# A depthwise convolution as three half-rate filters, written over its own input, on VectorE beside a matmul stream

## The chip, the cores and the metric

The kernel runs on one core of a Trainium2 chip. The metric is the device time of one execution in microseconds (us). Before the change three runs took 2227.54, 2218.27 and 2216.67 us; the median is 2218.27 us.

## The reference, cut to what matters

One layer on a sequence of 2048 frames with 1024 channels, all in float32: a norm, a combined input projection, two branches, a gated merge, an output projection and an MLP. The convolution sits in branch B.

```
proj = rmsnorm(x) @ w_in
u_pool, u_glu, g_a, g_b = split(proj)
branch_a = pool_mixer(u_pool, ...)            # trailing means, small matmuls
v = a * sigmoid(gate)                         # a, gate: halves of u_glu, 512 channels each
v = depthwise_conv(v, conv_w, width 31, causal) + conv_b
branch_b = silu(layernorm(v)) @ w_conv_out
merged = sigmoid(g_a) * branch_a + sigmoid(g_b) * branch_b
x = x + rmsnorm(merged @ w_o)
x = x + rmsnorm(relu(rmsnorm(x) @ w_up)^2 @ w_down)
```

Depthwise means that each channel has its own 31 taps: y[n] is the sum over k of w[k] times v[n + k], on a v with 30 zeros in front.

## The kernel before

Channels lie on the 128 partitions and frames along the free dimension. The sequence is two blocks (b = 0, 1) of 1024 frames. The large matmuls take each float32 operand as a high and a low part (`split`, `split_w`: ScalarE rounds the high part, VectorE subtracts) and multiply octets of blocks with seven products in place of eight (`Octet`), so VectorE also adds and subtracts weights and cells (`ws`, `wl`, `tr`, `big` in the profile), and adds matmul results that lie in PSUM to a held copy (`block_out`, L119 to L116 in the profile; for instance `tr<-ga,tr`). There are three PSUM buffers for the main products (`ps_mm`). A product that needs a buffer, or an accumulator, that such an addition still reads has to wait for it.

TensorE runs one main line of products: input projection of block 0 (glu, pool, ga, gb), branch A of block 0, input projection of block 1, branch B and `wo` of block 0, branch A of block 1, the MLP's `up` of block 0, then the same rest for block 1 and the `down` products.

Everything else is background work in `Lane` objects. After each product the main line calls `bg()`, and each lane takes `rate` steps of its generators. The convolution is such a generator (`conv_steps`, L896): for each of four channel groups c of a block it loads a window `v` of 1054 frames from DRAM (`vd`), then runs 31 taps on VectorE over 1024 frames, one instruction per tap and one step per tap, into an accumulator `acc` in a one-buffer pool `p_y` (named `y` in the profile). It stores `acc` to `yd`, adds it to `sums`, and goes on. That is 32 steps a group, and eight groups in all: group 0 of block 0 beside glu, pool and ga of block 0, the others up to the MLP's `up` of block 0. The pool branch (`pool_steps`) uses the same two buffers of `v` windows. Each of SyncE's loads and stores (`load`, L125) stands in one queue in program order.

The instruction order of each engine is settled when the kernel is built: a scheduler places the background instructions between those of the main line, by priorities (`tc.high_priority`) and by an order that `behind()` and `marks` tie to the main line. An engine runs its own list strictly in order.

Of the kernel before, what the change touches and what calls it, by code (L numbers as in the profile page):

```python
# [8 lines left out]
F32 = mybir.dt.float32  # L9
# [6 lines left out]
P = 128  # L16
D = 1024
SEQ = 2048
T = 512
# [24 lines left out]
C_MPRE = 32  # L44
C_MPOST = 40
C_CNT = 48
C_CW = C_CNT + 4 * HALO
NCONST = C_CW + CC * TAPS


# [15 lines left out]
def block_kernel(  # L66
# [35 lines left out]
    def mk(pl, tag, dt=F32, shape=(P, TB)):  # L102
        return pl.tile(list(shape), dt, tag=tag, name=nm(tag))
# [79 lines left out]
    inv_d = p_const.tile([P, 1], F32, tag="invd", name="inv_d")  # L183
    nc.gpsimd.memset(inv_d, 1.0 / D)
    inv_c = p_const.tile([P, 1], F32, tag="invc", name="inv_c")
    nc.gpsimd.memset(inv_c, 1.0 / CW)


# [705 lines left out]

    sums, done = {}, set()

    def conv_steps(b, groups, ahead=True):


        def get(c):  # L900
            v = window(TAPS - 1 + TB)
            load(v, vd[c][:, b * TB : b * TB + TAPS - 1 + TB])
            return v

        v = None
        for c in groups:
            if v is None:
                v = get(c)
                yield 1
            nv = None  # L910
            acc = mk(p_y, "y")
            for k in range(TAPS):
                wk = col(C_CW + c * TAPS + k)
                if k == 0:
                    nc.vector.tensor_scalar(
                        acc, v[:, :TB], wk, col(C_CB + c), op0=ALU.mult, op1=ALU.add
                    )
                else:
                    nc.vector.scalar_tensor_tensor(  # L919
                        acc, v[:, k : k + TB], wk, acc, op0=ALU.mult, op1=ALU.add  # L920
                    )
                if ahead and k == 15 and c != groups[-1]:
                    nv = get(c + 1)
                yield
            v = nv
            if c == 0:
                sums[b] = mk(p_ss, "sm")
                nc.vector.tensor_copy(sums[b], acc)
            else:
                add(sums[b], sums[b], acc)  # L930
            load(yd[b, c, 0], acc)
            yield

    def norm_steps(b, lag):
# [68 lines left out]
    def pool_steps(b, alone):  # L1003

        def get(g):
            s, u = window(W), tr()
            load(s, ud[g][:, b * TB : b * TB + W])
            load(u, ud[g][:, HALO + b * TB : HALO + b * TB + TB])
            return s, u

        s, u = get(0)
        yield 1
        for g in range(CC):
            w, m = WINDOWS[g], 1
            while m < w:
                lo = HALO - (w - 2 * m)
                s2 = window(W) if alone or m in (2, 8) else mk(p_ss, "r", F32, (P, W))
                add(s2[:, lo:], s[:, lo:], s[:, lo - m : W - m])
                s, m = s2, 2 * m
                yield  # L1020
            if b == 0:
                mul(
                    s[:, HALO : HALO + w],
                    s[:, HALO : HALO + w],
                    cst[:, C_CNT + g * HALO : C_CNT + g * HALO + w],
                )
# [502 lines left out]

    clear_halos()  # L1530
    opening()
    tail = Lane(1.9, conv_steps(0, (0,)))
    stats = Lane(1, in_stats(1))

    def then(f, o, at=4):
# [9 lines left out]
        return o  # L1545

    def after_glu():
        ahead[0] = AHEAD
        lanes.append(tail)

    def more():
        pool_weight()
        tail.gens.append(chain_of(pool_steps(0, True), conv_steps(0, (1, 2, 3), False)))
        tail.rate = 3

    pi = pool_in(0, parts)[0]
    run_first(o1, then(lambda: lanes.append(stats), then(after_glu, o2, 6)), bg, dve)
# [18 lines left out]
        yield from gen  # L1576

    rest = [marked(chain_of(*rest), "conv")]
    lanes += [Lane(3.2, *rest, marked(norm_steps(0, 1), "norm"))]

    def pooling():
        lanes[0].rate = 2.8
        lanes.append(Lane(1.7, pool_steps(1, False)))
        lanes.append(Lane(1.5, behind_all(conv_steps(1, (0, 1, 2, 3)), "conv", ("windows", 1))))


    pi = pool_in(1, parts)[0]
# [10 lines left out]
    lanes.append(conv1)  # L1598
    merged = merge(0, bg)
    fetched = []  # L1600
    conv1.rate = 6
    parts = Parts(lambda ops: token_parts(ops, lambda c, t: parts.raw(c, t), *BIG, TR))
    chain = out_proj(
        0, merged, ((0,), (1,)), bg, parts.some, lambda: fetched.extend(fetch_spread(mxd, 1))
# [487 lines left out]
```

## Time and profile before

| what | value |
|---|---|
| profiled execution, its own time | 2218.92 us |
| its span, first to last instruction | 2217.1 us |
| median of the three runs | 2218.27 us |
| TensorE (PE) busy | 2166.1 us, 98% of the span |
| VectorE (DVE) busy | 1686.0 us, 76% |
| ScalarE (ACT) busy | 1052.7 us, 47% |
| mean granted TensorE clock | 0.991 |
| convolution taps on DVE | 240 at 1281 ns and 8 at 810 ns |

The profiled execution is 1.8 us longer than its span and 0.65 us longer than the median. A busy share is a mean over stages. In the rows below "idle before" or a bracket at a row's end tells how long the engine stood before the instruction, and who ended that wait.

### The profile page before, as it was taken

The page shows a single profiled execution, that of the slowest core. Times are in us where ns is not written, and L with a number is a line of the kernel's source. Part 1 is how long each engine was busy: PE and PEld are TensorE (multiplying, and loading weights), DVE is VectorE, ACT ScalarE, POOL GpSimd, SP SyncE. Part 2 cuts the span into 40 slices and gives each one's busy share as a digit, 9 for nine tenths or more (in the row PEclk, how much of TensorE's full clock was granted, in tenths as well). Part 3 has the DMA queues.
Part 4 walks back from the last instruction along what each step waited for, and adds up shares of the span by engine and source line. Part 5 has one row for each costly group of instructions (what it writes and reads, how often), then busy time and mean ns, then how long its engine had stood idle before and what let it go on. Part 6 is the DMA issues. An engine that isn't in the chain of part 4 may idle for free. (4 is left out here: it accounts for less than half of the span.)

```text
span 2217.1 us, 25074 instructions
## 1 busy us (share of the span) xinstructions
PE 2166.1 (98%) x9576; PEld 1786.1 (81%) x9576; DVE 1686.0 (76%) x1637; ACT 1052.7 (47%) x1094; POOL 27.3 (1%) x51
## 2 busy tenths in 40 slices
PE   9999999999999999999999999999999999999996
PEld 7787888788788787888888877888878888888875
DVE  8897788998688899878757857876655556696767
ACT  6444454334543445445635766655454222223553
POOL 1000000000000000000000000000000000000001
PEclk9999999999999999999999999999999999999997
DMA  7678997778897787345786677985956545446788
GB/s 270 239 267 305 335 351 267 263 249 293 324 380 241 257 306 294 124 154 201 279 297 246 238 274 267 340 321 211 351 206 230 181 158 189 147 146 223 270 300 255
DMA packets 158264, 568.04 MB, mean 256 GB/s; under 512 B 17696, under 2 KB 17952, under 8 KB 158112
## 3 DMA queue, kind: packets, MB, share of 16 engines
q1 hardware_dynamic: 140608, 503.43, 63.7%
q10 hardware_dynamic: 12672, 46.14, 5.3%
q0 software_dynamic: 4864, 16.87, 2.8%
q8 instruction: 75, 1.23, 0.2%
q14 instruction: 45, 0.37, 0.0%
HBM read 378.58 MB, written 188.84 MB: 256 GB/s over the span
## 5 line engine op out<-in xcount | busy, mean ns | idle before, releaser
L266 PE MATMUL up<-big,wh 128*128 128x512 f32 x1792 | 482.2, 390 | 6.0 <-DVE tr L116 4.2
L266 PEld LDWEIGHTS up<-big,wh 128*128 128x128 f32 x1792 | 336.5, 188 | 78.5 <-DVE tr L116 5.0
L223 ACT CAST wh<-wr 128x1024 fp32r<-128x1024 f32 x177 | 185.9, 1052 | 321.3 <-PE up L266 76.7
L266 PE MATMUL down<-tr,wh 128*128 128x512 f32 x800 | 312.0, 390 | 0.0
L919 DVE SCALAR_TENSOR_TENSOR y<-v,cst,y 128x1024 f32<-128x1024 f32 x240 | 307.4, 1281 | 2.8
L266 PE MATMUL down<-fo,wh 128*128 128x512 f32 x784 | 302.2, 390 | 1.2 <-ACT fo L1761 1.2
L266 PE MATMUL up<-big,wl 128*128 128x512 f32 x896 | 277.1, 390 | 0.0
L266 PE MATMUL down<-fo,wl 128*128 128x512 f32 x768 | 236.7, 389 | 3.5 <-DMA wl<-lows 3.5
L223 ACT CAST wh<-ws 128x1024 fp32r<-128x1024 f32 x118 | 124.1, 1052 | 209.6 <-PE up L266 69.2
L266 PEld LDWEIGHTS up<-big,wl 128*128 128x128 f32 x896 | 168.6, 188 | 34.9
L116 DVE TENSOR_TENSOR big<-big,down 128x1024 f32<-128x1024 f32 x88 | 106.9, 1219 | 115.5 <-PE down L266 107.0
L1761 ACT CAST fo<-tr 128x1024 fp32r<-128x1024 f32 x86 | 86.8, 1051 | 210.4 <-PE down L266 134.3
L266 PEld LDWEIGHTS down<-tr,wh 128*128 128x128 f32 x800 | 150.6, 188 | 31.2
L119 DVE TENSOR_TENSOR wl<-ws,wh 128x1024 fp32r<-128x1024 f32 x110 | 134.4, 1221 | 52.7 <-ACT wh L223 52.6
L266 PEld LDWEIGHTS down<-fo,wh 128*128 128x128 f32 x784 | 147.5, 188 | 32.1 <-ACT fo L1761 1.7
L266 PEld LDWEIGHTS down<-fo,wl 128*128 128x128 f32 x768 | 144.3, 188 | 33.9 <-DMA wl<-lows 4.0
L119 DVE TENSOR_TENSOR wl<-wr,wh 128x1024 fp32r<-128x1024 f32 x100 | 121.9, 1220 | 27.2 <-ACT wh L223 27.0
L119 DVE TENSOR_TENSOR tr<-tr,fo 128x1024 fp32r<-128x1024 f32 x86 | 101.8, 1220 | 46.8 <-ACT fo L1761 46.8
L266 PE MATMUL glu<-big,wh 128*128 128x512 f32 x464 | 126.3, 393 | 3.5 <-DVE tr L116 2.8
L266 PE MATMUL wo<-big,wh 128*128 128x512 f32 x480 | 128.7, 390 | 0.0
L266 PE MATMUL ga<-big,wh 128*128 128x512 f32 x448 | 120.0, 389 | 3.0 <-DVE tr L116 3.0
L266 PE MATMUL gb<-big,wh 128*128 128x512 f32 x448 | 121.5, 393 | 0.3 <-ACT tr L888 0.3
(194 smaller groups left out, 3362.0 us busy)
## 6 DMA issues: line engine op xcount, KB each, us to landing
tr<-fd SPq DMA_DIRECT2D x110, 512.0 KB, 4.5
wl<-kept SPq DMA_DIRECT2D x85, 512.0 KB, 4.5
kept<-wl SPq DMA_DIRECT2D x72, 512.0 KB, 6.0
wr<-w_down SPq DMA_DIRECT2D x68, 512.0 KB, 5.0
wr<-w_up SPq DMA_DIRECT2D x64, 512.0 KB, 4.7
wr<-w_in SPq DMA_DIRECT2D x60, 512.0 KB, 4.8
fd<-tr ACTq DMA_DIRECT2D x54, 512.0 KB, 3.5
fd<-tr SPq DMA_DIRECT2D x48, 512.0 KB, 3.0
```

The lines of the kernel that those rows point to most:

```text
L116: return nc.vector.tensor_tensor(o, a, b, op=ALU.add)
L119: return nc.vector.tensor_tensor(o, a, b, op=ALU.subtract)
L223: nc.scalar.copy(hi[:, :n], src[:, :n])
L266: i = nc.tensor.matmul(ps, w[wp][:, (at + k) * P : (at + k + 1) * P], rhs[k][xp], start=start and n == 0, stop=stop and n == len(order) - ...
L919: nc.vector.scalar_tensor_tensor(acc, v[:, k : k + TB], wk, acc, op0=ALU.mult, op1=ALU.add)
L1761: nc.scalar.copy(hi, t)
```

## The change

The 31 taps are split by parity. With ve and vo the even and odd frames of the window, E the 16 even taps on ve and O the 15 odd taps on vo, the even outputs are E + O. The odd outputs are the filter of the sums (w[2j] + w[2j-1]) on ve + vo, less E and the shifted O. So three filters of 16, 15 and 16 taps run over 512 or 513 frames each, where one of 31 taps ran over 1024. The sources ve and vo are every second float of the window (a step of two elements); the accumulators are dense. The outputs are written into the window itself, interleaved, so `acc` only holds the partial sums, and the store to `yd` and the addition to `sums` read `v`. A group has 47 scalar_tensor_tensor instructions, two tensor_scalar and one addition of 527 elements in 26 steps. The sums of taps are made once, in one instruction (`pair_taps`). The lanes' rates are lowered.

```
+    def pair_taps():
+        w = cst[:, C_CW:].rearrange("p (c k) -> p c k", c=CC)
+        nc.vector.scalar_tensor_tensor(
+            pair.rearrange("p (c k) -> p c k", c=CC), w[:, :, 1::2], -1.0, w[:, :, 2::2],
+            op0=ALU.mult, op1=ALU.subtract,
+        )
...
-            acc = mk(p_y, "y")
-            for k in range(TAPS):
-                wk = col(C_CW + c * TAPS + k)
-                if k == 0:
-                    nc.vector.tensor_scalar(
-                        acc, v[:, :TB], wk, col(C_CB + c), op0=ALU.mult, op1=ALU.add
-                    )
-                else:
-                    nc.vector.scalar_tensor_tensor(
-                        acc, v[:, k : k + TB], wk, acc, op0=ALU.mult, op1=ALU.add
-                    )
-                if ahead and k == 15 and c != groups[-1]:
+            acc = mk(p_y, "y", F32, (P, TB + 2))
+            odd, even = acc[:, : T + 1], acc[:, T + 2 :]
+            vs = v.rearrange("p (n k) -> p k n", k=2)
+            ve, vo = vs[:, 0], vs[:, 1]
...
+            nc.vector.tensor_scalar(even, ve[:, :T], wk(0), None, op0=ALU.mult)
+            nc.vector.tensor_scalar(odd, vo[:, : T + 1], wk(1), None, op0=ALU.mult)
+            yield
+            for j in range(1, HALF):
+                tap(even, ve[:, j : j + T], wk(2 * j))
+                if 2 * j + 1 < TAPS:
+                    tap(odd, vo[:, j : j + T + 1], wk(2 * j + 1))
+                if ahead and j == 8 and c != groups[-1]:
                     nv = get(c + 1)
                 yield
...
+            add(vo, ve, vo)
+            nc.vector.scalar_tensor_tensor(
+                ve[:, :T], odd[:, :T], col(C_CB + c), even, op0=ALU.add, op1=ALU.add
+            )
+            yield
+            nc.vector.scalar_tensor_tensor(
+                even, odd[:, 1:], col(C_CB + c), even, op0=ALU.subtract, op1=ALU.add
+            )
+            for j in range(HALF - 1, 0, -1):
+                tap(even, vo[:, j : j + T], pair[:, c * (HALF - 1) + j - 1 :][:, :1])
+                if j % 2:
+                    yield
+            nc.vector.scalar_tensor_tensor(
+                vo[:, :T], vo[:, :T], wk(0), even, op0=ALU.mult, op1=ALU.subtract
+            )
+            y, v = v[:, :TB], nv
...
-            load(yd[b, c, 0], acc)
+            load(yd[b, c, 0], y)
...
-    tail = Lane(1.9, conv_steps(0, (0,)))
+    tail = Lane(1.6, conv_steps(0, (0,)))
...
-        tail.rate = 3
+        tail.rate = 2.5
...
-    lanes += [Lane(3.2, *rest, marked(norm_steps(0, 1), "norm"))]
+    lanes += [Lane(2.7, *rest, marked(norm_steps(0, 1), "norm"))]
...
-    conv1.rate = 6
+    conv1.rate = 4
...
-    conv1.rate = 1.2
+    conv1.rate = 1.0
...
-        conv1.rate = 2.8
+        conv1.rate = 2.4
```

The lanes of block 1's convolution and of the pooling stage go from 1.5 to 1.3 and from 2.8 to 2.4. The table of the pool branch's counts at the sequence start is packed tighter (26 columns in place of 64), and two constants share a tile.

The scheduler places the background instructions anew. On VectorE, between the first two matmul results of block 0's gate ga (y is the accumulator, v the window, wl and ws weights), there stand before:

```order
L116 TENSOR_TENSOR tr_1503<-ga_1354,tr_1464 128x1024
L919 SCALAR_TENSOR_TENSOR y_971<-v_930,cst,y_971 128x1024
L119 TENSOR_TENSOR wl_1617<-wr_1614,wh_1616 128x1024
L919 SCALAR_TENSOR_TENSOR y_971<-v_930,cst,y_971 128x1024
L116 TENSOR_TENSOR ws_1702<-wr_1698,wr_1700 128x1024
L919 SCALAR_TENSOR_TENSOR y_971<-v_930,cst,y_971 128x1024
L116 TENSOR_TENSOR tr_1542<-ga_1141,tr_1381 128x1024
```

and after the change:

```order
L116 TENSOR_TENSOR tr_1520<-ga_1368,tr_1480 128x1024
L929 SCALAR_TENSOR_TENSOR y_972<-v_931,pair,y_972 128x512
L119 TENSOR_TENSOR wl_1637<-wr_1634,wh_1636 128x1024
L929 SCALAR_TENSOR_TENSOR y_972<-v_931,pair,y_972 128x512
L116 TENSOR_TENSOR ws_1722<-wr_1718,wr_1720 128x1024
L929 SCALAR_TENSOR_TENSOR y_972<-v_931,pair,y_972 128x512
L116 TENSOR_TENSOR tr_1562<-ga_1149,tr_1395 128x1024
```

Three taps over 1024 frames have become three over 512, at the same places.

On VectorE, between two results of block 1's pool product (tr and big are cells of the input of block 1, sm the running sum of the convolution's outputs), there stand before:

```order
L116 TENSOR_TENSOR tr_3185<-pool_3077,tr_3150 128x1024
L919 SCALAR_TENSOR_TENSOR y_2422<-v_2385,cst,y_2422 128x1024
L119 TENSOR_TENSOR tr_3199<-big_2614,tr_2871 128x1024
L919 SCALAR_TENSOR_TENSOR y_2422<-v_2385,cst,y_2422 128x1024
L119 TENSOR_TENSOR big_3202<-tr_3199,big_3201 128x1024
L116 TENSOR_TENSOR sm_1607<-sm_1607,y_2422 128x1024
L119 TENSOR_TENSOR tr_3205<-big_2616,tr_2908 128x1024
L116 TENSOR_TENSOR tr_3235<-pool_2920,tr_3102 128x1024
```

and after:

```order
L116 TENSOR_TENSOR tr_3215<-pool_3103,tr_3177 128x1024
L929 SCALAR_TENSOR_TENSOR y_2522<-v_2478,pair,y_2522 128x512
L119 TENSOR_TENSOR tr_3229<-big_2632,tr_2889 128x1024
L929 SCALAR_TENSOR_TENSOR y_2522<-v_2478,pair,y_2522 128x512
L119 TENSOR_TENSOR tr_3235<-big_2634,tr_2926 128x1024
L929 SCALAR_TENSOR_TENSOR y_2522<-v_2478,pair,y_2522 128x512
L119 TENSOR_TENSOR big_3232<-tr_3229,big_3231 128x1024
L929 SCALAR_TENSOR_TENSOR y_2522<-v_2478,pair,y_2522 128x512
L119 TENSOR_TENSOR big_3238<-tr_3235,big_3237 128x1024
L929 SCALAR_TENSOR_TENSOR y_2522<-v_2478,pair,y_2522 128x512
L116 TENSOR_TENSOR tr_3265<-pool_2938,tr_3128 128x1024
```

Two long taps and the addition to the running sum have gone, five short taps and one more subtraction have come.

On VectorE, where branch A of block 1 begins (ws, tr and big get the low parts of its cells; the last row is the total of squares that TensorE's rb matmul waits for), there stand before:

```order
L919 SCALAR_TENSOR_TENSOR y_5765<-v_5504,cst,y_5765 128x1024
L119 TENSOR_TENSOR tr_5858<-tr_5858,big_5857 128x1024
L919 SCALAR_TENSOR_TENSOR y_5765<-v_5504,cst,y_5765 128x1024
L119 TENSOR_TENSOR tr_5861<-tr_5861,big_5860 128x1024
L919 SCALAR_TENSOR_TENSOR y_5765<-v_5504,cst,y_5765 128x1024
L119 TENSOR_TENSOR big_5877<-big_5337,big_5876 128x1024
L119 TENSOR_TENSOR big_5886<-big_5416,big_5885 128x1024
L122 TENSOR_TENSOR tr_5988<-A_6000,tr_5988 128x1024
L116 TENSOR_TENSOR tr_5656<-tr_5656,tr_5951 128x1024
L919 SCALAR_TENSOR_TENSOR y_5765<-v_5504,cst,y_5765 128x1024
L116 TENSOR_TENSOR tr_5656<-tr_5656 128x512
```

and after:

```order
L119 TENSOR_TENSOR tr_5963<-tr_5963,big_5962 128x1024
L119 TENSOR_TENSOR tr_5966<-tr_5966,big_5965 128x1024
L119 TENSOR_TENSOR big_5982<-big_5430,big_5981 128x1024
L119 TENSOR_TENSOR big_5991<-big_5511,big_5990 128x1024
L116 TENSOR_TENSOR tr_5757<-tr_5757,tr_6056 128x1024
L119 TENSOR_TENSOR big_6076<-big_5590,big_6075 128x1024
L122 TENSOR_TENSOR tr_6096<-A_6108,tr_6096 128x1024
L116 TENSOR_TENSOR tr_5757<-tr_5757 128x512
```

The convolution's taps have gone from this place; they stand elsewhere in the list. TensorE's own list is the same but for the small matmuls of the pool branch and of the norms, which move by up to some 75 places; from branch B of block 1 on, VectorE's and TensorE's lists have the same instructions in the same order as before.

## Rows read from the trace of the kernel before

**Rows 1.** The page: busy us (share of the span) xinstructions of each engine.
```profile
PE 2166.1 (98%) x9576; PEld 1786.1 (81%) x9576; DVE 1686.0 (76%) x1637; ACT 1052.7 (47%) x1094; POOL 27.3 (1%) x51
```

**Rows 2.** Stretches: length, busy us (xcount) per engine, granted clock, DMA share, GB/s.
```profile
95.00:980.00 885.00, 870.84 (x3838) 718.20 (x3839) 763.18 (x710) 398.08 (x413) 8.88 (x16) 0.99 0.76 277
...
480.00:540.00 60.00, 60.00 (x267) 49.61 (x266) 55.06 (x47) 26.29 (x27) 0.00 (x0) 1.00 0.73 263
...
1080.00:1140.00 60.00, 60.00 (x267) 49.67 (x266) 34.58 (x30) 30.95 (x31) 0.00 (x0) 1.00 0.71 257
```

**Rows 3.** Waits of TensorE: us in total, times, longest us.
```profile
PE rb L550 <- DVE tr L116: 4.3, 3, 2.0
PE up L266 <- DVE tr L116: 4.2, 2, 2.9
...
PE glu L266 <- DVE tr L116: 2.8, 2, 1.4
PE gb L266 <- DMA wl<-kept: 2.0, 1, 2.0
...
PE A L266 <- DVE tr L119: 0.9, 1, 0.9
```

**Rows 4.** VectorE's groups by shape: busy us, mean ns | idle before, releaser.
```profile
L919 DVE SCALAR_TENSOR_TENSOR y<-v,cst,y 128x1024 f32<-128x1024 f32 x240 | 307.4, 1281 | 2.8
...
L116 DVE TENSOR_TENSOR tr<-tr 128x512 f32<-128x512 f32 x12 | 8.2, 687 | 0.1
L781 DVE SCALAR_TENSOR_TENSOR big<-big,cst,r 128x512 f32<-128x512 f32 x12 | 8.2, 746 | 1.6 <-ACT r L774 1.6
...
L915 DVE TENSOR_SCALAR y<-v,cst 128x1024 f32<-128x1024 f32 x8 | 6.5, 810 | 3.4 <-DMA yd<-y 3.1 <-DMA v<-vd 0.3
...
L594 DVE SCALAR_TENSOR_TENSOR sy<-s,sy 128x4 f32<-128x4 f32 x24 | 3.9, 161 | 0.7
```

**Rows 5.** Order of time around the ga wait, VectorE: start us, us, instruction.
```profile
166.99 1.23 DVE L116 TENSOR_TENSOR tr<-ga,tr 128x1024 f32<-128x1024 f32 x1
168.13 1.28 DVE L919 SCALAR_TENSOR_TENSOR y<-v,cst,y 128x1024 f32<-128x1024 f32 x1
169.32 1.22 DVE L119 TENSOR_TENSOR wl<-wr,wh 128x1024 fp32r<-128x1024 f32 x1
...
173.99 1.22 DVE L116 TENSOR_TENSOR tr<-ga,tr 128x1024 f32<-128x1024 f32 x1
```

**Rows 6.** The same around the ga and pool waits, TensorE.
```profile
175.35 1.63 PE L266 MATMUL ga<-big,wh 128*128 128x512 f32 x6 [2.96 <-DVE tr L116]
...
397.48 1.62 PE L266 MATMUL pool<-big,wh 128*128 128x512 f32 x6 [1.52 <-DVE tr L116]
```

**Rows 7.** Around the pool wait, VectorE.
```profile
388.03 1.22 DVE L116 TENSOR_TENSOR tr<-pool,tr 128x1024 f32<-128x1024 f32 x1
...
396.12 1.22 DVE L116 TENSOR_TENSOR tr<-pool,tr 128x1024 f32<-128x1024 f32 x1
```

**Rows 8.** The start of branch A of block 1, VectorE.
```profile
765.04 1.21 DVE L119 TENSOR_TENSOR tr<-tr,big 128x1024 fp32r<-128x1024 f32 x1
...
772.04 1.23 DVE L122 TENSOR_TENSOR tr<-A,tr 128x1024 f32<-128x1024 f32 x1 [2.23 <-DMA tr<-sad]
...
775.51 0.68 DVE L116 TENSOR_TENSOR tr<-tr 128x512 f32<-128x512 f32 x1
```

**Rows 9.** TensorE's wait for that total.
```profile
776.34 1.02 PE L550 MATMUL rb<-inv_d,tr 128*128 128x1 f32 x8 [2.03 <-DVE tr L116]
```

**Rows 10.** TensorE before and after its wait in the `up` products.
```profile
881.46 1.52 PE L266 MATMUL up<-big,wh 128*128 128x512 f32 x6
...
887.21 2.62 PE L266 MATMUL up<-big,wh 128*128 128x512 f32 x6 [2.87 <-DVE tr L116]
```

**Rows 11.** The stretches of 5 us around that wait, columns as in Rows 2.
```profile
885.00:890.00 5.00, 2.79 (x7) 2.22 (x8) 5.00 (x5) 2.31 (x3) 0.00 (x0) 0.76 0.02 9
```

**Rows 12.** DMA issues: queue, count, KB each, median us to landing.
```profile
yd<-y SPq DMA_DIRECT2D x8, 512.0 KB, 3.0
```

More of the change, by code (lines that the diff above doesn't have):

```diff
@@ L46 @@
 C_CNT = 48
-C_CW = C_CNT + 4 * HALO
+C_CW = C_CNT + sum(w - 1 for w in WINDOWS)
 NCONST = C_CW + CC * TAPS
@@ L182, in block_kernel @@
     nc.gpsimd.memset(f32(ones), 1.0)
-    inv_d = p_const.tile([P, 1], F32, tag="invd", name="inv_d")
+    inv = p_const.tile([P, 2], F32, tag="inv", name="inv")
+    inv_d, inv_c = inv[:, :1], inv[:, 1:]
     nc.gpsimd.memset(inv_d, 1.0 / D)
-    inv_c = p_const.tile([P, 1], F32, tag="invc", name="inv_c")
     nc.gpsimd.memset(inv_c, 1.0 / CW)
@@ L895, in block_kernel @@
     sums, done = {}, set()
+    HALF = (TAPS + 1) // 2
+    pair = p_const.tile([P, CC * (HALF - 1)], F32, tag="pair", name="pair")
+    def pair_taps():
[4 more added lines that the diff above has]
+        )
     def conv_steps(b, groups, ahead=True):
@@ new lines, in conv_steps, with tap, wk @@
+            odd, even = acc[:, : T + 1], acc[:, T + 2 :]
+            vs = v.rearrange("p (n k) -> p k n", k=2)
+            ve, vo = vs[:, 0], vs[:, 1]
+            def tap(o, src, w):
+                nc.vector.scalar_tensor_tensor(o, src, w, o, op0=ALU.mult, op1=ALU.add)
+            def wk(k):
+                return col(C_CW + c * TAPS + k)
+            nc.vector.tensor_scalar(even, ve[:, :T], wk(0), None, op0=ALU.mult)
+            nc.vector.tensor_scalar(odd, vo[:, : T + 1], wk(1), None, op0=ALU.mult)
@@ L923, in conv_steps @@
+            yield
[4 more added lines that the diff above has]
+                if ahead and j == 8 and c != groups[-1]:
                     nv = get(c + 1)
                 yield
-            v = nv
+            add(vo, ve, vo)
+            nc.vector.scalar_tensor_tensor(
+                ve[:, :T], odd[:, :T], col(C_CB + c), even, op0=ALU.add, op1=ALU.add
+            )
@@ L926, in conv_steps @@
             if c == 0:
                 sums[b] = mk(p_ss, "sm")
-                nc.vector.tensor_copy(sums[b], acc)
+                nc.vector.tensor_copy(sums[b], y)
             else:
-                add(sums[b], sums[b], acc)
-            load(yd[b, c, 0], acc)
+                add(sums[b], sums[b], y)
+            load(yd[b, c, 0], y)
             yield
@@ L1021, in pool_steps @@
             if b == 0:
[L1022 to L1026, printed above, removed]
+                at = C_CNT + w - 2 - g
+                mul(s[:, HALO :][:, : w - 1], s[:, HALO :][:, : w - 1], cst[:, at : at + w - 1])
             nc.vector.scalar_tensor_tensor(
@@ L1547, in after_glu @@
     def after_glu():
+        pair_taps()
         ahead[0] = AHEAD
@@ L1578, in block_kernel @@
     rest = [marked(chain_of(*rest), "conv")]
-    lanes += [Lane(3.2, *rest, marked(norm_steps(0, 1), "norm"))]
+    lanes += [Lane(2.7, *rest, marked(norm_steps(0, 1), "norm"))]
     def pooling():
-        lanes[0].rate = 2.8
+        lanes[0].rate = 2.4
         lanes.append(Lane(1.7, pool_steps(1, False)))
-        lanes.append(Lane(1.5, behind_all(conv_steps(1, (0, 1, 2, 3)), "conv", ("windows", 1))))
+        lanes.append(Lane(1.3, behind_all(conv_steps(1, (0, 1, 2, 3)), "conv", ("windows", 1))))
     pi = pool_in(1, parts)[0]
@@ L2051, in octets @@
         return np.stack([np.stack(q) for q in o]).transpose(0, 1, 3, 2, 4, 5).reshape(-1, 4, P, D)
-    counts = np.stack(
-        [w / np.minimum(np.arange(1, HALO + 1, dtype=np.float32), w) for w in WINDOWS]
-    ).astype(np.float32)
+    counts = np.concatenate([w / np.arange(1, w, dtype=np.float32) for w in WINDOWS])
     params = np.concatenate(
@@ L2065 @@
             cols(g["norm_mlp_post"]),
-            np.broadcast_to(counts.reshape(1, -1), (P, 4 * HALO)),
+            np.broadcast_to(counts.astype(np.float32)[None], (P, counts.size)),
             g["conv_w"].reshape(TAPS, CC, P).transpose(2, 1, 0).reshape(P, CC * TAPS),
```

## The prediction

> **What bounds the kernel now.** I read the page's busy times first, then the stretches, then TensorE's waits, and last the order of time at the longest of these. TensorE is busy for 2166.1 of 2217.1 us, VectorE for 1686.0 [rows 1]. Is TensorE's pace set by VectorE? Two stretches of 60 us say no: with VectorE busy for 55.06 us and with 34.58 us TensorE did 267 matmuls, that is one per 0.225 us [rows 2]. So VectorE's load costs time only where TensorE stands still for it. The whole convolution lies between 95 and 980 us; there TensorE is busy for 870.84 of 885 us and stands for 14.2 us [rows 2]. That is the pool from which this change can pay, plus what the clock gives back: after the 2.87 us wait in the `up` products six matmuls took 2.62 us where six took 1.52 before [rows 10], in a stretch whose granted clock is 0.76 [rows 11], so 1.1 us on top of the wait.
>
> TensorE's waits name VectorE's additions and norms, and one DMA [rows 3]. Some of this is a floor: an addition that TensorE needs at once takes 1.2 us by itself [rows 5], and the two glu waits are at most 1.4 us long [rows 3]. Only what is beyond about 1.3 us a wait is queueing behind other VectorE work.
>
> **VectorE's work.** Out go 240 taps at 1.281 us (307.4) and 8 first taps at 0.810 us (6.5), 313.9 us in all [rows 4]. In come 8 groups of 47 taps over 512 or 513 frames. The nearest row is another scalar_tensor_tensor over 512 with a column of `cst` as its scalar, at 0.746 us [rows 4]: 376 x 0.746 = 280.5 us. The 16 new first taps lie between half of the old one, 0.405, and a whole short tap, 0.746; I take 0.5 as they have one scalar column less: 8.0 us (6.5 to 11.9). The 8 additions of 527 frames are near the 0.687 us of 512 [rows 4], with a little more for length 0.70: 5.6 us. `pair_taps` runs once and costs between 0.16 us (a tiny instruction [rows 4]) and 0.75. Sum 294.3, so VectorE's busy time falls by 19.6 us (16 to 21), to about 1666. Since an instruction starts a little before the one ahead of it ends (a long tap's successor 1.19 us after it, 168.13 to 169.32 [rows 5]; I estimate 0.66 for a short tap, 1.19 less the 0.535 by which the two rows differ), the time on VectorE's list falls by more, 240 x 1.19 - 376 x 0.66 = 37 us, less some 6 that the other new instructions take beyond the old first taps: near 30.
>
> Two halves of a tap cost 2 x 0.746 - 1.281 = 0.21 us more than a whole [rows 4], and this speaks against the change. [...]
>
> The sources are read at a step of two floats, and no row shows that. From below, it costs nothing (the dense row); from above each of the 400 new instructions takes 512 more cycles' worth, the 0.535 us by which a 1024 tap exceeds a 512 one: 214 us. I take nothing, since the row with the same operation and operands is the dense one, and keep the top for a rival.
>
> **What of it reaches TensorE,** place by place.
> - The ga wait, 2.96 us at 175.35 [rows 6]. VectorE goes without a pause from one ga addition (166.99) to the next (173.99) [rows 5], with three long taps between. They become three short ones: 3 x (1.19 - 0.66) = 1.6 us. The wait falls to its floor of 1.3: -1.6.
> - The pool wait, 1.52 us at 397.48 [rows 6], is at its floor already, and here VectorE gets more to do between 388.03 and 396.12 [rows 7]: two long taps and the addition to the running sum go, five short taps and a subtraction come, 5 x 0.66 - 2 x 1.19 = +0.9.
> - Branch A of block 1. `tr<-tr,big` at 765.04 [rows 8] frees A's wait of 0.9 us [rows 3]; five long taps stand among its predecessors and go, so that wait goes. But `tr<-A` then stands for the DMA of the gate until 772.04 [rows 8], which the taps don't move, and the total of squares ends at 776.2 (775.51 + 0.68). With one tap and one addition fewer in between it ends 2.3 us sooner; TensorE's rb matmul, which waits 2.03 us for it [rows 9], stands 9 matmuls earlier, 9 x 0.225 = 2.0. So the gain lies between 0.3 us (gate as late as now) and 4.0 (0.9 + 2.03 + 1.1 of clock, gate early); I take -1.5, nearer the row of the DMA.
> - There the small spread matmuls come 12 matmuls, 2.7 us, behind the rb ones, in place of some 60. VectorE's chain between them is one subtraction of 1.14 and eleven tiny instructions at 0.161 [rows 4] and gaps: 3.2 us. A new wait of 0 to 1: +0.5.
> - The `up` wait, 2.87 us [rows 10]: one tap ahead of the addition gets shorter, -0.5, from 0 (a weight's DMA decides) to -1.6 (floor).
> - The wait for `wl<-kept`, 2.0 us [rows 3] and its 1.1 of clock. SyncE's list is rearranged around it, since block 0's norm moves by some 57 matmuls. From -3.1 (gone) to +3 (another like it); I take half of the price, -1.5.
> - Elsewhere in the stretch taps stand ahead of additions that TensorE needs some products later, and this cover stays. From branch B of block 1 on the lists are the same: 0.
>
> Sum: -1.6 + 0.9 - 1.5 + 0.5 - 0.5 - 1.5 = -3.7 us. The profiled execution takes 2218.92, so 2215.2; it is 0.65 above the median of the runs, so 2214.5.
>
> **The rivals.**
> *VectorE's slack empties the whole stretch.* 30 us less on a list that is busy for 763.18 of 885 us [rows 2] may move every addition, and every store and load behind it, ahead of its need. For it: nearly all of TensorE's waits here name VectorE [rows 3]. Against: the floor, and the gate's DMA [rows 8]. Price: about 11 of the 14.2 us and three clock losses of 1.1: -14, 2204.
> *The store now reads the window.* A window's buffer was free at the last tap; now it is free when `yd` has landed, 3.0 us after issue [rows 12]. There are two buffers, shared with the pool branch, and the next load of one stands in SyncE's single queue: while it waits, the weight loads behind it wait too. If each store delays a weight by its 3.0 us past TensorE's need, that is 3.0 + 1.1 of clock, 4.1 us. It decides from four of the eight groups on: 4 x 4.1 - 3.7 = +12.7, 2231. Against it: SyncE's loads run several products ahead, and only one wait on a weight's low part shows here, of 2.0 us [rows 3].
> *The step of two halves the rate.* Then the list grows by 214 - 30 = 184 us where 885 - 763.18 = 122 are free [rows 2], and 62 us overflow onto TensorE: 2280. [...]
> *Nothing moves.* VectorE gets its 20 us back and TensorE waits as long as before, at other places: 2218.
>
> **How the numbers follow.** About 0.5%, 11 us, is what a measurement of this kernel can tell from no change. The forecast has 0.60, with a range of its own of 2208 to 2219; nothing moves 0.09; the slack rival 0.20; the store 0.08; the step 0.03. Faster by over 0.5% (below 2207) is the slack rival: 0.20. Within is forecast and nothing: 0.69. Slower is store and step: 0.11. The range holds 8 in 10 when it reaches 2204 below, the middle of the slack case, and 2226 above, which takes in two stores that delay weights (2 x 4.1 on 2218) and leaves out the step and the worse half of the store.
>
> **What would show it.** Right: 376 short taps at 0.74 to 0.75 us, VectorE's busy time near 1666, a ga wait near 1.3 us, the A wait gone, and TensorE busy for a little more than 870.84 of those 885 us. Wrong: taps of a microsecond or more (the step), TensorE's waits on `wl<-kept` or `wr` loads after a store of `yd` (the store), or a standing time in this stretch of 5 us or less (the slack rival).

## The result, and the profile after

The changed kernel takes 2231.0 us (median of 8 runs, 2226.0 to 2237.0) where the kernel before takes 2218.4 in runs on the same chip: a ratio of 1.0049, 95% interval 1.0032 to 1.0067. It is slower by 0.49%; the forecast was 2214.5, faster. Its profiled execution has a span of 2229.6 us, 12.5 longer than before.

VectorE did what was worked out. The page's busy times answer to [rows 1], VectorE's groups by shape (busy us, mean ns | idle before) to [rows 4]:

```profile
PE 2176.6 (98%) x9576; PEld 1791.3 (80%) x9576; DVE 1654.3 (74%) x1790; ACT 1051.0 (47%) x1094; POOL 27.0 (1%) x51
```
```profile
L929 DVE SCALAR_TENSOR_TENSOR y<-v,pair,y 128x512 f32<-128x512 f32 x120 | 89.9, 750 | 1.8
L929 DVE SCALAR_TENSOR_TENSOR y<-v,cst,y 128x512 f32<-128x512 f32 x120 | 89.7, 748 | 0.0
L929 DVE SCALAR_TENSOR_TENSOR y<-v,cst,y 128x513 f32<-128x513 f32 x112 | 84.1, 751 | 0.0
...
L951 DVE SCALAR_TENSOR_TENSOR y<-y,cst 128x512 f32<-128x512 f32 x8 | 6.0, 749 | 0.1
L116 DVE TENSOR_TENSOR v<-v 128x527 f32<-128x527 f32 x8 | 5.6, 703 | 0.0
...
L936 DVE TENSOR_SCALAR y<-v,cst 128x513 f32<-128x513 f32 x8 | 3.9, 485 | 0.0
```

A short tap costs 0.748 to 0.751 us, the forecast's 0.746, with its source at a step of two floats; the same operation with dense operands, from `y` to `y`, costs 0.749. VectorE is busy for 31.7 us less, TensorE for 10.5 us more. The stretch that answers to [rows 2] (columns as there) holds 41 matmuls fewer than before, with 44 us less of VectorE, and TensorE is busy in it for 4.1 us less, not for a little more:

```profile
95.00:980.00 885.00, 866.76 (x3797) 711.70 (x3796) 719.10 (x848) 390.58 (x408) 8.64 (x16) 0.99 0.76 275
```

The longest waits of TensorE (us in total, times, longest), against [rows 3]: `tr` for `rb` has grown from 2.0 to 4.7, the wait of ga is 2.8 as it was 3.0, and waits of branch B, on `big`, are new.

```profile
PE rb L550 <- DVE tr L116: 5.5, 2, 4.7
PE up L266 <- DVE tr L116: 4.0, 2, 2.7
...
PE ga L266 <- DVE tr L116: 2.8, 1, 2.8
...
PE down L266 <- DMA wl<-lows: 2.3, 1, 2.3
...
PE B L266 <- DVE big L119: 1.4, 2, 0.8
```

**Where the time lies.** TensorE issues the same 9240 product matmuls in both programs. So the start of the k-th of them can be set against the start of the k-th before, and a stretch of the program is longer or shorter by the change of that difference. Us against the first trace of before; "again" is a second trace of the same program (runs b2 and a2 below):

| place, about (us) | before again | changed | changed again | e2 | e9 |
|---|---|---|---|---|---|
| ga wait, 155-182 | +1.7 | +2.7 | +2.0 | -1.1 | +2.6 |
| end of ga, start of gb of block 1, 515-592 | -2.2 | -1.4 | +1.6 | -0.9 | -3.9 |
| start of branch B of block 0, 612-638 | +0.7 | +3.3 | +1.6 | +1.9 | -0.1 |
| branch A of block 1, 753-805 | -0.5 | +4.7 | +5.1 | -1.4 | -1.6 |
| fo sums (VectorE's additions on `fo` that an rb matmul waits for), 1335-1405 | +3.5 | +3.3 | +0.4 | +3.4 | +0.1 |
| down, 1565-1635 | +2.8 | +3.1 | +3.1 | -0.7 | +2.1 |
| wl<-lows, 2125-2156 | -3.2 | -2.9 | -3.1 | -0.4 | -0.7 |
| last products, 2156-2190 | +1.6 | +1.6 | +1.6 | +1.6 | +0.1 |
| all others | -2.9 | -0.9 | -0.9 | +0.5 | +3.5 |
| sum to the last product | +1.5 | +13.5 | +11.5 | +2.8 | +2.2 |

The traced executions took 2219.5, 2231.4, 2228.8, 2221.0 and 2220.0 us in the order of the columns, the first trace of before 2218.9; that of e2 lies 4.9 below its median.

Two places stand out of what the kernel before does by itself: branch B and, with 5 us, branch A. Against the second trace of before the two traces of the changed kernel have 7.0 and 5.5 us more of standing TensorE, and 5.0 and 4.5 us more of busy TensorE for the same matmuls; the mean granted clock is 0.987 and 0.988, where the second trace of before has 0.989 and the first 0.991. Against that first trace it is 3.7 and 2.2 of standing and 9.8 and 9.3 of busy, so how much of the loss is waits and how much clock depends on the trace that one compares with.

**Branch A of block 1.** `sad` holds the gate of branch A in DRAM, `x1d` takes the sum `x` behind the out projection, `xt` is the input x. Order of time in the changed kernel: GpSimd's queue, then SyncE's, VectorE and TensorE.

```profile
756.60 0.53 POOL L129 DMA_DIRECT2D x1d<-big  x1 [0.60 <-DVE big L116]
764.16 0.55 POOL L129 DMA_DIRECT2D big<-xt  x1 [7.03 <-PE wo L266]
764.88 1.18 POOL L129 DMA_DIRECT2D big<-xt  x2 [0.17 <-PE wo L266]
766.45 0.54 POOL L129 DMA_DIRECT2D big<-xt  x1 [0.39 <-issue]
...
769.51 1.84 SPq L125 DMA_DIRECT2D tr<-sad  x4
...
767.71 1.22 DVE L119 TENSOR_TENSOR tr<-tr,big 128x1024 fp32r<-128x1024 f32 x1 [4.33 <-ACT big L1086]
...
779.89 1.23 DVE L122 TENSOR_TENSOR tr<-A,tr 128x1024 f32<-128x1024 f32 x1 [3.21 <-DMA tr<-sad]
781.03 0.68 DVE L116 TENSOR_TENSOR tr<-tr 128x512 f32<-128x512 f32 x1
...
781.86 1.19 PE L550 MATMUL rb<-inv,tr 128*128 128x1 f32 x5 [4.74 <-DVE tr L116]
```

Before, the fourth store of `x1d` and the four 512 KB loads of `x` behind it on that queue came after the gate loads:

```profile
785.01 0.53 POOL L129 DMA_DIRECT2D x1d<-big  x1 [30.61 <-DVE sy L594]
785.67 0.55 POOL L129 DMA_DIRECT2D big<-xt  x1
...
766.64 2.15 SPq L125 DMA_DIRECT2D tr<-sad  x4
```

With the filter steps gone from here, VectorE reaches the fourth `big<-big,big` so early that its store goes 28 us sooner (756.60, not 785.01). GpSimd, which stood 30.61 us ahead of that store before, now stands 7.03 us for a product of `wo` and issues the `x` loads at 764 to 767, ahead of the gate loads, which the next product on VectorE wants at once. The mean busy share of the DMA engines over these twenty microseconds is 1.03 in the changed kernel, where it was 0.69 and then 0.84 before (stretches, second to last column; changed, then before):

```profile
760.00:770.00 10.00, 9.12 (x39) 7.02 (x38) 4.14 (x5) 5.93 (x8) 2.18 (x4) 1.00 1.03 419
770.00:780.00 10.00, 6.64 (x28) 4.80 (x26) 5.67 (x6) 6.37 (x8) 0.00 (x0) 1.00 1.03 409
780.00:790.00 10.00, 8.14 (x31) 7.03 (x32) 5.99 (x16) 1.05 (x1) 0.00 (x0) 0.66 0.54 199
```
```profile
760.00:770.00 10.00, 9.03 (x39) 6.85 (x38) 9.81 (x9) 8.25 (x10) 0.00 (x0) 1.00 0.69 250
770.00:780.00 10.00, 7.97 (x37) 6.34 (x36) 7.08 (x9) 1.71 (x2) 0.00 (x0) 0.92 0.84 320
```

So `tr<-A` stands for its gate until 779.89 (772.04 before [rows 8]), the total of squares stands behind it in VectorE's order, and TensorE's wait of 2.03 [rows 9] becomes 4.74, followed by ten microseconds at a mean clock of 0.66. A's own wait, which was to go with the taps ahead of `tr<-tr,big`, is there still: VectorE now stands 4.33 us for a cast of ScalarE's, and TensorE 0.76 and 0.47 in place of 0.9.

**The ga wait.** Three shorter taps did shorten VectorE's list between the two ga additions, but VectorE then stands for the store `kept<-wl`, which still reads the buffer that the next `wl` goes to:

```profile
169.57 1.23 DVE L119 TENSOR_TENSOR wl<-wr,wh 128x1024 fp32r<-128x1024 f32 x1 [1.40 <-DMA kept<-wl]
...
173.18 1.22 DVE L116 TENSOR_TENSOR tr<-ga,tr 128x1024 f32<-128x1024 f32 x1
...
174.45 2.93 PE L266 MATMUL ga<-big,wh 128*128 128x512 f32 x6 [2.83 <-DVE tr L116]
```

Before, the same instruction stood for nothing (169.32 [rows 5]). Up to here six of the traces below have one and the same order on TensorE, VectorE and ScalarE. VectorE stands 0.22 to 3.40 us there (in e2 for ScalarE, in the others for that store), and TensorE waits 1.43 longer than VectorE stands in each: 1.65 (e13), 1.86 (e2), 2.83 and 3.26 (the changed kernel twice), 3.23 (e8), 4.83 (e1).

**Branch B of block 0.** `zd` holds the normed output of the convolution in DRAM, the input of branch B. The last `zd` store of block 0's norm comes at 620.33 (608.95 before), 11 us later, and the casts of `zd` on ScalarE, 628.75 to 633.88, wait for their loads when the first product needs them:

```profile
620.33 0.32 SPq L125 DMA_DIRECT2D zd<-tr  x1
621.18 2.80 SPq L125 DMA_DIRECT2D big<-zd  x4
...
633.88 1.05 ACT L1086 CAST big<-big 128x1024 fp32r<-128x1024 f32 x1 [0.21 <-DMA big<-zd]
...
634.98 0.50 PE L266 MATMUL B<-big,wh 128*128 128x512 f32 x1 [0.77 <-DVE big L119]
```

The rates were lowered by 14 to 17% here, but only the filter has fewer steps; pooling and norm, on the same lanes, have as many as before. The last filter of block 0 is stored 8 us later already (535.63 against 527.57).

### The profile page after: what moved, and what is told of

Read it like the earlier page. It is cut to its first block, busy times and chain, and to the rows that moved or that the text cites. A ratio compares the mean times of both kernels' runs of the same rounds, so it can differ in the third digit from the quotient of the medians.

```text
span 2229.6 us, 25222 instructions
## 1 busy us (share of the span) xinstructions
PE 2176.6 (98%) x9576; PEld 1791.3 (80%) x9576; DVE 1654.3 (74%) x1790; ACT 1051.0 (47%) x1094; POOL 27.0 (1%) x51
## 5 line engine op out<-in xcount | busy, mean ns | idle before, releaser
L929 DVE SCALAR_TENSOR_TENSOR y<-v,cst,y 128x512 f32<-128x512 f32 (+1 forms) x232 | 159.9, 749 | 0.0
```

Source lines behind the costliest of these rows:

```text
L929: nc.vector.scalar_tensor_tensor(o, src, w, o, op0=ALU.mult, op1=ALU.add)
```

## The experiments

Each run asks which of three theories holds. *Order*: the filter costs what it should; the lanes' steps moved, and with them sums, stores and loads, which makes a few waits of TensorE and the clock behind them. *Filter*: the taps at a step of two floats, or the store out of the window, cost the time. *Clock*: the waits are no worse than before and the granted clock falls by chance. Each median stands with the ratio to runs of the kernel before on the same chip.

| run | median us | ratio, 95% interval |
|---|---|---|
| e1 changed, out projection at 6 | 2231.5 | 1.0059 (1.0039 to 1.0078) |
| e2 changed, x loads behind gates | 2225.9 | 1.0026 (1.0007 to 1.0045) |
| e3 before, out projection at 4 | 2220.1 | 1.0003 (0.9985 to 1.0020) |
| e5 changed, all old rates | 2229.2 | 1.0043 (1.0027 to 1.0058) |
| e6 before, all new rates | 2314.8 | 1.0438 (1.0418 to 1.0457) |
| e7 e2 + tail at 3 | 2227.6 | 1.0042 (1.0027 to 1.0056) |
| e8 e2 + lane 0 at 3, 2.6 | 2234.2 | 1.0078 (1.0063 to 1.0093) |
| e9 e7 + last rates 1.2, 2.8 | 2218.7 | 1.0000 (0.9987 to 1.0013) |
| e10 new filter in 32 steps, old rates | 2226.0 | 1.0037 (1.0023 to 1.0051) |
| e11 e10 + x loads behind gates | 2221.3 | 1.0019 (1.0005 to 1.0034) |
| e12 e9 + first rate 1.9 | 2221.6 | 1.0026 (1.0009 to 1.0044) |
| e13 e2 + last rates 1.2, 2.8 | 2224.0 | 1.0031 (1.0018 to 1.0043) |

**e2: the x loads behind the gate loads.** The edit, cut to its two sides:

```
-                    aside(x[c, t], xt[b, c, t])      # POOL's queue, at the end of out_proj
+                    load(x[c, t], xt[b, c, t])       # SP's queue, in roots(), second half only
```

> The changed kernel with the rate left at 4; only the four x loads of block 0's second half go to SP's queue, behind the first four gate loads of branch A of block 1, instead of to POOL's queue. Order theory: TensorE's wait ahead of rb falls from 4.74 to 1.5 to 2.5 us, VectorE's wait for the gate load (3.21) falls below 1, and the time is 2225 to 2228. If the wait were for VectorE's order and not for the transfer, the wait stays at 4 to 5 and the time at 2231. Filter theory: 2231 too. Clock theory: wait shorter, time 2224 to 2234.

Measured 2225.9, 5.1 below the changed kernel (the two intervals of the ratio overlap: 1.0032 to 1.0067 and 1.0007 to 1.0045). The gate loads go at 765.30, the first `x` load at 774.01, and TensorE's wait is 1.48:

```profile
774.35 1.02 PE L550 MATMUL rb<-inv,tr 128*128 128x1 f32 x8 [1.48 <-DVE tr L116]
```
```profile
765.30 2.08 SPq L125 DMA_DIRECT2D tr<-sad  x4
774.01 0.42 SPq L125 DMA_DIRECT2D big<-xt  x1
```

Nothing of VectorE's work was taken away, only the queue and the place of the four transfers. TensorE's order is the same in the whole program, VectorE's and ScalarE's up to 793 us, that is until behind this wait. So the transfers are the cause of the wait, as the order theory has it.

**e1: only the rate there put back.**

```
-    conv1.rate = 4
+    conv1.rate = 6
```

> The changed kernel with one number put back: the lane's rate in block 0's out projection is 6 again, not 4, so that filter steps stand on VectorE through branch A of block 1 and the fourth sum big<-big,big comes behind the first gate product, as before. Order theory (a few waits of TensorE that the moved order makes, and the clock behind them, are the loss; the filter itself costs nothing): the four x loads are issued behind the first gate loads, TensorE's wait ahead of rb in branch A falls from 4.74 to 1.5 to 2.5 us, the granted clock of the 10 us behind it rises above 0.75, the stretch is 4 to 5 us shorter, and the time is 2224 to 2228. Filter theory (taps on every other column, or the store out of the window, cost the time): within 2 us of 2231. Clock theory (where the clock falls is chance of the phase, not of the waits): the wait in branch A falls, but the time may lie anywhere from 2224 to 2234, with half clock at other places than in the changed kernel.

The wait went (1.27), the stretch is 0.2 us from before, and nothing was won: 2231.5. Some 60 us later TensorE waits 4.12 in the first `up` products. Filter steps now push the last gate product on VectorE back to 826.09 (823.38 in the changed kernel); its store `mad<-tr` (the gated result of branch A) holds SyncE's queue, and the weight of `up` stands behind it (829.60, in the changed kernel 825.76), then VectorE for that weight and TensorE for VectorE's sum:

```profile
822.35 5.30 SPq L125 DMA_DIRECT2D mad<-tr  x2
829.60 0.33 SPq L125 DMA_DIRECT2D wr<-w_up  x1
...
837.63 1.23 DVE L116 TENSOR_TENSOR ws<-wr,wr 128x1024 f32<-128x1024 f32 x1 [4.47 <-DMA wr<-w_up]
```
```profile
840.05 1.22 PE L266 MATMUL up<-big,wh 128*128 128x512 f32 x2 [4.12 <-DVE tr L116]
```

The time missed what the order theory expected, though the wait moved as it said: a wait taken away came back at another place. The traced execution is the fastest of the twelve, 2227.2.

**e3: the old filter with that one rate.** The edit of e1 the other way round, `conv1.rate = 6` to 4 in the kernel before.

> The kernel before, old filter of 31 taps, with one number changed: the lane's rate in block 0's out projection is 4, not 6. Order theory: the wait of branch A appears in the old filter as well: 4 to 5 us ahead of rb instead of 2.03, x loads issued ahead of the gate loads, and the time is 2221 to 2225, that is 3 to 6 above the kernel before. Filter theory: the old filter is not hurt, 2217 to 2220. Clock theory: the wait appears, the time is anything from 2216 to 2226.

The wait appears in the old filter too, 4.77 us, with the `x` loads at 757.69 to 759.98 ahead of the gate loads at 764.33, and its stretch is 2.9 longer. The time, 2220.1, can't be told from before, and lies just below what was expected of the order theory: 2.5 us of this trace are given back at 875 to 900. So the wait by itself need not cost the program 5 us.

```profile
774.00 1.19 PE L550 MATMUL rb<-inv_d,tr 128*128 128x1 f32 x5 [4.77 <-DVE tr L116]
```

**e5 and e10: the new filter under the old rates** (1.9, 3, 3.2, 2.8, 1.5, 6, 1.2, 2.8 for 1.6, 2.5, 2.7, 2.4, 1.3, 4, 1.0, 2.4), e10 also in as many steps as the old one:

```
-                if ahead and j == 8 and c != groups[-1]:
+                if ahead and j == 15 and c != groups[-1]:
...
-            yield                     # between the two sums
...
-                if j % 2:
-                    yield
+                yield                 # one step for each tap of the third filter
```

> The new filter with all eight old rates (1.9, 3, 3.2, 2.8, 1.5, 6, 1.2, 2.8): the lanes take as many steps at a place as before, and since a group has fewer steps they run ahead. Order theory: with branch A's filter steps back and block 0's norm as early as before, the waits at the start of branch B (0.95, 0.63, 0.77) and ahead of rb in branch A (4.74) go back to those of before, 2216 to 2224. Filter theory: still 2228 to 2234, since every tap is the same. Clock theory: 2218 to 2234, with half clock at places that neither trace showed.

> The new filter cut into as many steps per group as the old one (32 instead of 26: one step for each tap of the third filter, none between the two sums, the next window's load at the 16th step as before), with all eight old rates; so the lanes stand at the same places of the program as in the kernel before, and what differs is that a step costs VectorE less. Order theory: the waits added at branch B and in branch A go (B below 1.6, ahead of rb 1.5 to 2.5), none as in run e5 (4.05 at 394.87) appears, and the time is within 4 us of the kernel before: 2214 to 2222. Filter theory: 2228 to 2234 as in the changed kernel. Clock theory: 2216 to 2230, with the waits gone.

e5, 2229.2: branch B's waits are gone (last `zd` store at 569), and waits of 4.05, 2.05 and 1.72 us come in glu of block 1 (395 to 428). In branch A the `x` loads are behind the gate loads, and ahead of rb TensorE still waits 3.35, now for VectorE's own order, with taps up to the gate product at 783.02. e10, 2226.0, is above the 2222 that the order theory allowed. Its branch B is clear (+0.5), but branch A is worse than in the changed kernel, by the same mechanism:

```profile
759.34 0.55 POOL L129 DMA_DIRECT2D big<-xt  x1
...
763.58 1.63 SPq L125 DMA_DIRECT2D tr<-sad  x3
...
774.63 1.23 DVE L122 TENSOR_TENSOR tr<-A,tr 128x1024 f32<-128x1024 f32 x1 [5.79 <-DMA tr<-sad]
...
776.60 1.83 PE L550 MATMUL rb<-inv,tr 128*128 128x1 f32 x8 [7.60 <-DVE tr L116]
```

So the rate of 4 is enough for the collision (e3), but it isn't needed: with as many steps and the old rates the shorter taps by themselves let VectorE reach the fourth sum early. I had put the collision down to the rate alone; this corrects it.

**e11: e10 with the edit of e2.**

> Run e10 (new filter in 32 steps, all old rates) with the x loads of block 0's second half on SP's queue behind the first gate loads, the edit of run e2. In e10 TensorE waited 7.60 ahead of rb, with the x loads issued at 759.34 to 761.41 and the gate loads at 763.58. Order theory: that wait falls to 1.5 to 2.5 and the clock behind it rises, the other waits (4.38 at 419 in glu) stay, and the time is 5 to 7 below e10: 2219 to 2221. If the wait were for VectorE's own order, it stays and the time is 2226. Clock theory: wait gone, 2219 to 2227.

2221.3, 4.7 below e10 (4.0 by the ratios to the kernel before, as the two ran on different chips), just above what was expected; the wait is 3.80, not 1.5 to 2.5, as `tr<-A` still stands 2.00 for its gate. TensorE's order is again the same in the whole program. So two pairs of kernels that differ by this edit alone give 5 and 4 us, each with intervals that overlap a little.

**e7, e8, e9, e12, e13: e2 with other rates.** The lines, with the runs that change each:

```
-        tail.rate = 2.5
+        tail.rate = 3                                  # e7, e9, e12
-    lanes += [Lane(2.7, ...   and   lanes[0].rate = 2.4
+    lanes += [Lane(3, ...     and   lanes[0].rate = 2.6      # e8
-    conv1.rate = 1.0          and   conv1.rate = 2.4
+    conv1.rate = 1.2          and   conv1.rate = 2.8         # e9, e12, e13
-    tail = Lane(1.6, ...
+    tail = Lane(1.9, ...                               # e12
```

> Run e2 (x loads behind the gate loads) with one rate more put back: the lane of block 0's pooling and its last three filters goes at 3 again, not 2.5 (pooling has as many steps as before, so the lower rate only made it later). Order theory: block 0's norm ends 10 to 40 us earlier, its last zd store comes before 612 instead of at 616 to 620, the waits ahead of branch B (in e2 1.41 at gb for wl<-kept and the casts of zd behind it, 1.9 us in all; 3.3 in the changed kernel) go, and the time falls 1.5 to 3.5 below e2's 2225.9, to 2222 to 2224.5. Rival (work only moved): filter steps that come earlier stand in the way of VectorE's sums for glu or ga of block 1, as with all old rates, where TensorE waited 4.05 at 394.87; then 2226 to 2232. Clock theory: B's wait goes and the time stays at 2226, give or take 3, with half clock elsewhere.

> Run e2 with the lane of block 0's last filters and its norm at 3 and then 2.6, where the changed kernel has 2.7 and 2.4 and the kernel before 3.2 and 2.8. Order theory: the lists up to the pool stretch of block 1 stay those of e2; the norm ends 6 to 12 us earlier, the last zd store comes at 606 to 612, branch B starts without a wait, and the time is 2222 to 2224.5. Rival (work only moved): more filter steps per product in glu and ga of block 1 bring a wait of 1 to 4 us between 395 and 530; 2225 to 2230. Clock theory: waits go, time 2223 to 2229.

> Run e7 (x loads behind the gate loads, tail lane at 3) with the last two rates put back as well: 1.2 and 2.8 in the up product, where e7 has 1.0 and 2.4. In e7 TensorE waits 4.27 at 1031 for ScalarE's copy of an up product, which stands behind the squares of block 1's norm there. Order theory: the norm of block 1 comes some 5 to 15 us earlier, this wait falls below 1 (or moves to a place of its own with another size), and the time is 2221 to 2225. Rival (work only moved): another wait of 2 to 5 us appears between 880 and 1040; 2226 to 2231. Filter theory: 2227.5 as e7.

> Run e9 (2218.7: x loads behind the gate loads, rates 3, 1.2 and 2.8 put back) with the first rate put back too: 1.9 for the first filter, not 1.6. At ga e9 waits 3.93 (the changed kernel 2.83); both runs with 1.9 waited less there, 2.68 in two waits (e5) and 1.36 (e10). Order theory: the wait of ga falls by 1.5 to 2.5 with the clock behind it full, the rest stays, and the time is 2214 to 2218, the first below the kernel before. Rival (work only moved): the filters of block 0 come earlier still and a wait of 2 to 5 us appears in glu or ga of block 1 (395 to 530); 2219 to 2224. Clock theory: 2214 to 2222.

> Run e2 (x loads behind the gate loads) with the last two rates put back to 1.2 and 2.8, the tail's rate left at 2.5. If the last two rates carry e9's gain: 2219 to 2222, the waits of branch B (1.9) still there. If the tail's rate of 3 carries it (through branch B): 2224 to 2227, as e2. Clock theory: 2219 to 2228.

In e7 and e8 the last `zd` store comes at 596 and 608 (616 in e2) and branch B's waits went, as expected, and the time didn't fall. e8 has a wait of 6.25 in glu at 424, and both have a new one of 4.27 at 1031, behind the last filter, where block 1's norm now stands ahead of ScalarE's copy of an `up` product:

```profile
1031.40 2.07 PE L266 MATMUL up<-big,wh 128*128 128x512 f32 x4 [4.27 <-ACT tr L428]
```

With the last two rates put back as well (e9) that wait is gone too, and the time, 2218.7, is that of the kernel before, a little better than expected. The last two rates alone (e13, 2224.0) leave branch B's waits (1.62 and 0.76). e12 waits 2.28 in all at ga, where e9 waits 3.93, but 1.55 at 538, 0.88 and 1.78 in gb and 2.78 at the fo sums are new against e9: 2221.6, the rival. Against e9 the intervals overlap (1.0009 to 1.0044 and 0.9987 to 1.0013), and the ga wait varies by 3 us between traces of one order.

e9 speaks against the filter theory: with the same taps, the same stores out of the window and VectorE 33 us less busy than before (1653.1) it runs in the time of the old filter. It differs from the kernel before by the place of the `x` loads too; the old filter with that edit was not run, but there the `x` loads come behind the gate loads anyway (785.67). No run was faster than the kernel before.

**e6: the old filter under all new rates.**

> The old filter of 31 taps with all eight new rates (1.6, 2.5, 2.7, 2.4, 1.3, 4, 1.0, 2.4). A group still has 32 steps here, so the lanes fall behind. If the rates alone make the loss: norm of block 0 ends later than in the changed kernel (last zd store behind 620), branch B waits 2 to 6 us, and the time is 2226 to 2236. If the loss comes from the shorter filter and the rates only follow it: 2217 to 2223, with branch A at 2 us since filter steps are left over for it. Clock theory: 2217 to 2230.

2314.8, far beyond the 2226 to 2236 that I allowed. The old filter needs 32 steps per group where the rates reckon with 26; the norms of both blocks end too late, and branch B stands for `zd`:

```profile
662.78 0.79 PE L266 MATMUL B<-big,wh 128*128 128x512 f32 x1 [15.62 <-ACT big L1053]
```
```profile
1211.06 0.80 PE L266 MATMUL B<-big,wh 128*128 128x512 f32 x1 [28.33 <-ACT big L1053]
```

The two starts of branch B make 85 of the 98 us by which this trace's last product is later (36 and 48 by the same reckoning as in the table). This is the branch B mechanism at full size, and it shows that rates this low were too low for anything but the shorter filter.

**a2 and b2: both programs once more,** nothing edited.

> The changed kernel once more, nothing edited, for a second trace of the same lists. Order theory: the same waits of TensorE at the same places within 1 us: 2.8 at ga, 1.4 to 2.4 around branch B, 4.7 ahead of rb in branch A, 1.8 ahead of rb<-inv,fo at about 1380, and half clock behind each of them as in the first trace; span 2226 to 2234. Clock theory: the waits are there, but the falls of the clock lie elsewhere: of the three places where the first trace lost 2.9 (ga), 1.6 (fo) and 2.9 (down) to the clock at least one shows none, and a place that was undisturbed shows one.

> The kernel before once more, nothing edited. Order theory: as its first trace, no half clock behind the wait at ga (2.96) nor at down (1.25 and 0.76), no wait ahead of branch B, 2.0 ahead of rb in branch A; span 2214 to 2221. Clock theory: the same waits within 1 us, but half clock at one or two places that the first trace shows at full clock, and full clock at one or two where it shows half; a span that differs by 2 to 8 us.

a2 took 2228.8, b2 2219.5. Branch A's wait is in a2 again (4.35), branch B's too (0.76, with 1.51 of gb earlier). But a wait of the same size costs the clock in one execution and not in the next. At ga, before waited 2.96 and then 2.97; the five microseconds behind it, first trace and second:

```profile
175.00:180.00 5.00, 4.65 (x21) 3.87 (x22) 5.00 (x7) 1.06 (x1) 0.00 (x0) 1.00 0.42 171
```
```profile
175.00:180.00 5.00, 5.00 (x17) 3.96 (x17) 5.00 (x8) 0.48 (x1) 0.00 (x0) 0.71 0.48 197
```

So what the traces of before and changed showed at ga, at the fo sums and at down (+2.7, +3.3, +3.1) can't be laid to the change: b2 has +1.7, +3.5 and +2.8 there, and a2 at the fo sums +0.4. The clock theory holds for these places, not for branch B's waits and the longer wait of branch A, which both traces of the changed kernel have and neither of before.

## Why the prediction was wrong, point by point

- *VectorE's work*: right. 376 short instructions at 0.748 to 0.752, 16 first taps at 0.485 (0.5 taken), 8 additions at 0.703 (0.70). Summed by durations that is 18.6 us less than the old filter (19.6 forecast). Busy time fell by 31.7, to 1654.3 and not to 1666, since short neighbours overlap: two taps take 1.41 us, 0.66 from start to start, as estimated. The "near 30" of the list was the right figure for busy time too.
- *The pool*: the premise that VectorE's load costs only where TensorE stands was borne out: e9 takes 33 us from VectorE and gains nothing. But the 14.2 us of standing were taken as something that can only shrink; in both traces of the changed kernel they are 18.
- *Branch A of block 1, -1.5, "the gain lies between 0.3 us and 4.0"*: this step failed, and it is the largest that the runs explain. It measured +4.7 and +5.1. The step treated the gate's DMA as fixed ("which the taps don't move"). The taps did move it: not the gate load, but the stores and loads on GpSimd's queue behind a sum of VectorE's, which then competed with it. Each moved instruction had been followed on VectorE and TensorE, not on that queue. The range had no side below nothing.
- *"Elsewhere in the stretch this cover stays. From branch B of block 1 on the lists are the same: 0"*: failed. At the start of branch B of block 0, which the sum didn't name, it measured +3.3 and +1.6, as the norm ends 11 us later under rates lowered for steps that it doesn't have fewer of. The 0 from branch B of block 1 on held: from 1116 us on, where the lists are the same, the two traces add 5.2 and 3.7, and before again adds 4.5.
- *The ga wait, -1.6*: failed in both traces, 2.8 and 3.3, by the same kind of step as branch A: a DMA that was not followed. VectorE's list got shorter, and VectorE stood for `kept<-wl` for 1.40 and 1.83 us; less that stand the wait is 1.43, close to the 1.3 that was taken as its floor. In e10 VectorE doesn't stand there and TensorE waits 1.36. *The wait for wl<-kept, -1.5*: it is gone in the changed kernel's first trace (the place has -1.4), but a2 has a wait of 1.51 on a copy of ScalarE's there (+1.6), and before again has -2.2 by itself.
- *The small terms* don't show. The pool wait (+0.9 forecast) is 0.87 and 1.38, before 1.52 and 0.90; the spread matmuls of branch A (+0.5) wait for nothing over 0.15; the `up` wait (-0.5) is 2.71 and 2.28, before 2.87 and 1.97.
- *The rivals*: the step of two is refuted by the rows of taps (0.748 to 0.751 us, where it needed a microsecond or more). The store rival gave 2231, which is the time, for the wrong reason: behind the eight stores of `yd` the trace shows two waits of VectorE for a window, 0.82 at 478.0 and 2.90 at 545.9, and TensorE stands for at most 0.46 within 5 us of them; e9, with all eight stores, loses nothing.
- *The numbers*: the 0.11 for slower was too small. The cases that led there were all properties of the new instructions; none was "the same work at another place collides", which the order of instructions already showed, in the sums that moved ahead at branch A.

That the loss is one of order and not of the filter's work rests on e9. What stays open is how the 12.6 us divide. The edit of e2 accounts for some 5, but e1 and e3, which take the same wait away and bring it in by a rate, change the time by nothing that is clear of noise. e9 recovers the other 7 by three rates; one rate alone (e7, +1.7 from e2) and the other two alone (e13, -1.9) gave no difference clear of noise. How much is waits and how much clock was not separated; single traces of one program differ by as much as 3 us at one place.

## What to carry to other kernels

Work taken from an engine that is off the critical path is not only free time: here it let what stood behind it on that engine come sooner, and with it a DMA that waited for it (the fourth store of `x1d`, at 756.60 and not at 785.01). Follow each moved instruction to the queue that it releases, and ask whose urgent load is in the air then. Ask too which DMA the next instruction on that engine will find unfinished: at ga the time won on VectorE went into standing for a store, 1.40 and 1.83 us in the two traces. Where steps of several kinds share a rate, a change of the count of one kind needs a rate of its own, and an expectation that a wait goes away needs the next wait behind it.

## What the hardware showed that I had not expected

- A source at a step of two floats costs nothing here: 0.748 to 0.751 us against 0.749 for the dense operation in the same trace and 0.746 for the dense row before [rows 4].
- The granted clock behind one and the same wait is not the same from one execution to the next: 1.00 and 0.71 in the five microseconds behind 2.96 and 2.97 us, in one program. Single executions of the kernel before spread from 2210.5 to 2231.0 us.
- Four 512 KB loads issued 3 to 5 us ahead of others on another queue delayed those: `tr<-A` stood for its gate until 10.4 us after the gate's issue (769.51 to 779.89), where before it was 5.4 (766.64 to 772.04), at a DMA share of 1.03 against 0.69 in the ten microseconds of the issue. With the four loads behind the gate's (e2) VectorE started `tr<-A` at 772.39, 7.1 us after the issue at 765.30, and stood for nothing there.
